# Weight pieces of 1024 columns in buffers of half the size, for a hybrid attention and convolution layer

## The chip, the core and the metric

The kernel runs on one core of one Trainium2 chip. The metric is device time in microseconds (us) of one execution; less is better. The core has a matrix engine (PE, whose weight loads are listed apart as PEld), a vector engine (DVE), a scalar engine (ACT), a general engine (POOL) and a queue that issues transfers (SP). Each takes its own instructions strictly in order, and semaphores tie them together. Transfers from all queues run on the same 16 DMA engines.

## The reference

One layer on 256 tokens of width 2048, all in float32, with batch 1 and depth 1:

```python
parts = split(x @ w_in)                        # q, k, v of 3 dilated groups, GLA's q, k, v, r, low, two gates
for g, dil in enumerate((1, 4, 16)):           # 8 heads of 128, span 128, T5 bias
    outs[g], lses[g] = dilated_group(q, k, v, bias, dil)
ya = (softmax(lses) * outs).sum() @ w_proj_a
log_a = log_sigmoid(g_low @ gla_gate_w + gla_gate_b) / 16
o = gla(gq, gk, gv, log_a)                     # 4 heads, chunks of 64
yb = (rms_norm(o) * gla_norm_g * silu(gr)) @ w_proj_b
x1 = layernorm(alpha * x + (sigmoid(m_a) * ya + sigmoid(m_b) * yb) @ w_out)
g = causal_conv3(x1 @ ffn_w_gate) + conv_b     # width 5632
out = layernorm(alpha * x1 + (silu(g) * (x1 @ ffn_w_up)) @ ffn_w_down)
```

Almost all of the work is x @ W with weights that are read once.

## The kernel before

**Pieces.** The host lays the weights out as a stream `wp` of pieces of 128 partitions x 2048 columns of float32 (1 MB each), in the order of `_stream`. `load` (L145 to L148) issues the transfer of one piece on SP, at L147. The PE multiplies float32 in a rounded form, so `split` (L135 to L137) makes two parts of each piece: ACT writes `hi`, a rounded copy (L136), and DVE writes `lo = raw - hi` (L137). A product of x and W is then three products, x_hi W_hi, x_lo W_hi and x_hi W_lo, summed in PSUM. `two_parts` and `piece` (L150 to L173) take the buffers.

**Buffers.** All are slots of 2048 columns: 2 of tag `raw` and 6 of tag `quarter` for loaded pieces, 3 of `whi` and 2 of `wlo` for the parts. A load can be issued when the piece that held its slot was read for the last time; for `raw` that is DVE's `lo`.

**Three ways to use a piece.**
- A *tile* (`b16`, L235): one piece holds 16 blocks of 128 columns as stationary operands. 16 matmuls of 512 columns use `hi` (L228), then 16 of 256 columns use `lo` (L230). The `gqk`, `qk`, `fg` and `fu` tiles are of this kind.
- A *chunk* (`chunk_step`, L264; `a_part`, L251): one piece holds four row blocks of 512 output columns, as moving operand, with 24 matmuls (L260, L261, L262). The `m`, `pb`, `yp`, `wo` and `wd` products are of this kind, with one piece for each step.
- A *unit* (`seven`, L312): a product of 256 rows in 2x2 blocks, with seven block products in place of eight. Each of the block products `p1` to `p7` uses two pieces and 24 matmuls (L329). Before `p5` and `p6` DVE adds pieces to pieces in place (`add`, L342); for `p7` and `p2` POOL issues adding transfers between buffers (`add_by_dma`, L345). There are 10 units in the mixer (`v`, `gv`, `gr`, `m`) and five in the feed-forward part (`fgu`).

**What sets the order.** The Python code names work in the order of use. In the mixer, steps of units are taken in turn with the tiles that make q and k; attention and GLA stages are put between them by `pump`. In the feed-forward part the blocks of 8, 8, 8, 8, 8, 4 row blocks (`FSPLIT`) run one after the other, and the `wd` steps of one block are put between the steps of the next one's unit. A scheduling layer then places the instructions of each engine, with its own estimate of when each can start, and adds the semaphores. So the order on ACT and DVE is close to that of the code, but not the same.

**Places that the prediction speaks of.** `vD`: in a unit, `p7` makes `u = s + E` (L378) and `c = D - u` (L379) on DVE, and `p3` then adds another product into the bank `D`, so PE waits for L379. `wd` after a unit: ACT copies the last bank of the unit (`c`, L398) and then splits the next `wd` piece. `fguA`: the second product into bank A, whose pieces ACT splits behind two transfers of `x1f` (L114) that ACT issues itself. `pa` (L982): the sum of a tile's two halves, which frees the tile's bank.

Of the kernel before, what the change touches and what calls it, by code (L numbers as in the profile page):

```python
# [11 lines left out]
F32 = mybir.dt.float32  # L12
# [22 lines left out]
NEG = -1e30  # L35
FSPLIT = (8, 8, 8, 8, 8, 4)


# [19 lines left out]
def hybrid_layer(ctx: ExitStack, tc: tile.TileContext, wp, xt, wgl, gw, par, relb, onehot, rows, xk, out):  # L58
# [91 lines left out]
    def two_parts(raw, spare=False):  # L150

        n_blk[0] += 1
        hi = wpool.tile([P, 2048], F32R, tag="quarter" if spare else "whi", name=f"whi_{n_blk[0]}", bufs=6 if spare else 3)
        lo = wpool.tile([P, 2048], F32R, tag="quarter" if spare else "wlo", name=f"wlo_{n_blk[0]}", bufs=6 if spare else 2)
        split(hi, lo, raw)
        return hi, lo

    def piece(i, before=(None,)):

        if len(before) == 1:  # L160
            return two_parts(load(i))
        raw = raw_tile(i)
        n_blk[0] += 1
        hi = wpool.tile([P, 2048], F32R, tag="whi", name=f"whi_{n_blk[0]}")
        lo = wpool.tile([P, 2048], F32R, tag="wlo", name=f"wlo_{n_blk[0]}", bufs=2)
        n = 2048 // len(before)
        for k, f in enumerate(before):
            if f is not None:
                f()
# [62 lines left out]

    by_cols = lambda ws: lambda kc: [a[:, kc * P : (kc + 1) * P] for a in ws]

    def b16(name, opnd, i, before=(None,)):  # L235
        return b_tile(name, by_cols(piece(i, before)), opnd, 16)

    def b16_three(names, opnd, idx):

        ws = [by_cols(two_parts(load(i), spare=(i == idx[-1]))) for i in idx]  # L240
        pss = [cbank(n) for n in names]
        for kc in range(16):
            for w, ps in zip(ws, pss):
                nc.tensor.matmul(ps, w(kc)[0], opnd(kc), start=(kc == 0), stop=False)
        for w, ps in zip(ws, pss):
            for kc in range(16):
                nc.tensor.matmul(ps[:, S:], w(kc)[1], opnd(kc)[:, :S], start=False, stop=(kc == 15))
        return pss
# [31 lines left out]
    def a_pair_by_half(name, opnd, idx):  # L280

        pcs = [piece(i) for i in idx]
        pss = [[cbank(f"{name}_t{t}") for t in range(2)] for _ in pcs]
        for t in range(2):
            for (hi, lo), ps in zip(pcs, pss):
                for k in range(4):
                    w = slice(k * 512, (k + 1) * 512)
                    a_part(ps[t], opnd(k), hi[:, w], lo[:, w], t, k == 0, k == 3)
        return pss
# [25 lines left out]
    def seven(name, xs, comb, i, store, by_dma=True):  # L315
# [7 lines left out]
        def part(ps, a, raw, p, first):  # L323

            hi, lo = two_parts(raw)
            for w, which in ((hi, 0), (hi, 1), (lo, 0)):
                for k in range(4):
                    kc = 4 * p + k
                    nc.tensor.matmul(  # L329
                        ps, a(kc)[which], w[:, k * 512 : (k + 1) * 512],  # L330
                        start=(first and w is hi and which == 0 and kc == 0),
                        stop=(w is lo and kc == 7), skip_group_check=not first,
                    )
# [13 lines left out]
        def get(k):  # L347
            return load(i + k, "quarter", 6)

        def p1():  # L350
            st["T"] = [get(0), get(1)]
            st["A"] = cbank(name + "A")
            product(st["A"], a11, st["T"])
            st["s"] = blk("s")
            nc.scalar.activation(st["s"], st["A"], AF.Copy)

        def p5():
            st["B12"] = [get(2), get(3)]
            for a, b in zip(st["T"], st["B12"]):
                add(a, b)  # L360
            st["D"] = cbank(name + "D")
            product(st["D"], z, st["T"])

        def p6():
            st["B22"] = [get(4), get(5)]
# [26 lines left out]
        def p2():  # L392
            st["B21"] = [get(6), get(7)]
# [4 lines left out]
            nc.scalar.activation(c, st["A"], AF.Copy)  # L398
            store(0, 0, c)
# [120 lines left out]
    def gkq(which, h):  # L520
        st = {}

        def f(j, before=(None,)):
            def g():
                ps = b16("gqk", xop, AT["gkq", which] + 2 * h + j, before)
                if not j:
                    st["b"] = blk("gqk")
                b_sum(ps, st["b"][:, j * S : (j + 1) * S])
                if j:
                    GKQ[which][h] = spill("gkqs", st["b"])  # L530
            return g
        return f

    def head(h):
# [3 lines left out]
        def f(g, which):  # L538
            def t():
                ps = b16("qk", xop, AT["qk", h] + 2 * g + which)  # L540
                if not which:
# [186 lines left out]
    def gkq_tiles():  # L728
        for which in range(2):
            for h in range(GH):  # L730
                f = gkq(which, h)
                yield f(0, [pair_of_x(j) for j in range(4)] if not which and not h else (None,))
                yield f(1)
# [102 lines left out]
    for n in range(2):  # L836
        pss = a_chunk("m", xop, 16, AT["mb"] + 4 * n, 2)
        for t in range(2):
# [3 lines left out]
    drain()  # L842
    home[:] = "quarter", 6
    early.close()
# [28 lines left out]
    for n in range(4):  # L873
        g = [gate(1, n, t) for t in range(2)]
        pss = a_chunk("pb", by_pairs(OB), 16, AT["pb"] + 4 * n)
        for t in range(2):
# [4 lines left out]
    for n in range(4):  # L881
        g = [gate(0, n, t) for t in range(2)]
        pss = a_chunk("yp", yop, 8, AT["pa"] + 2 * n)
        for t in range(2):
# [59 lines left out]
    for n in range(4):  # L944
# [3 lines left out]
        if n < 3:  # L948
            pss = a_chunk("wo", yt, 16, AT["wo"] + 4 * n)
            for t in range(2):  # L950
                residual(n, t, pss[t])
    pcs = [two_parts(load(AT["wo"] + 12 + k), spare=(k > 1)) for k in range(4)]
    for t in range(2):
        ps = cbank(f"wo_t{t}")
        for k0 in range(4):
            hi, lo = pcs[k0]
            for k in range(4):
                w = slice(k * 512, (k + 1) * 512)
                kc = 4 * k0 + k
                a_part(ps, yt(kc), hi[:, w], lo[:, w], t, kc == 0, kc == 15)  # L960
# [38 lines left out]
    def tile_group(f0, h):  # L999
# [3 lines left out]
        def gate_tile(f):  # L1003
            def g():
                if f == 0:
                    first = AT["fgu", 0]
                    st["three"] = dict(zip("gun", b16_three(("fg", "fu", "fg"), x1op, (first, first + 1, first + 2))))
                three = st.get("three", {})
# [4 lines left out]
        def up_tile(f):  # L1013
            def g():
                if f == 0:
                    ps = st["three"]["u"]
                elif f == 1:
                    with tc.issue_after(held.ins):
                        ps = b16("fu", x1op, AT["fgu", f] + 1)
                else:  # L1020
                    ps = b16("fu", x1op, AT["fgu", f] + 1)
                gated(h()[:, f % 4], st["c"], b_own(ps))
# [26 lines left out]
    def down_group(part, nf, hs):  # L1049
# [25 lines left out]
        def step(n, k0):  # L1075
            def g():
                at = AT["wd", part] + n * nf // 4
                if not k0:
# [17 lines left out]
        for n in range(0, 4, 2):  # L1096
            at = [AT["wd", part] + n + i for i in range(2)]
            if n == 2:
# [27 lines left out]

    home[:] = "raw", 2
    f0, older = 0, []
# [58 lines left out]
def _stream():  # L1187
# [129 lines left out]
```

## Time and profile before

| | |
|---|---|
| time, median of 3 runs | 1923.15 us (1919.91 to 1925.47) |
| the profiled execution, its own time | 1920.82 us |
| its span, first to last instruction | 1919.1 us |
| DVE, ACT, POOL busy | 1413.8, 1022.8, 179.6 us |
| mean granted PE clock | 0.985 |
| HBM read, written | 383.46 MB, 33.72 MB |
| transfers of pieces from HBM | 163 into `raw`, 160 into `quarter`, 1 MB each |

The profile lists busy time by engine, groups of instructions by line with their mean duration, waits (who waited for whom), a timeline, the time of DMA transfers, and the clock that the PE was granted, 1.00 being full speed. A busy PE is modelled: its matmuls overlap, so the pitch between them (0.227 us for 512 columns) is less than the 0.39 us that one is listed with. A wait is listed at the first instruction that could not start, with the instruction that released it.

### The profile page before, as it was taken

The numbers are of one execution on the slowest core, as the hardware profiler recorded it, in microseconds if no ns is written. First come the engines' busy times: TensorE is split into PE (matmuls) and PEld (weight loads), VectorE is DVE, ScalarE is ACT, GpSimd is POOL, SyncE is SP. The second block draws the span as 40 slices with busy tenths as digits, with TensorE's granted clock in tenths as the row PEclk, the third lists the DMA queues.
The fourth block names the chain that finished last, engine by engine and source line by source line (L and its number), as shares of the span: only waits on it lengthen the run. The fifth ranks groups of instructions, "written<-read, shape, count | busy, mean of one in ns | idle before, by whom it ended". The sixth has DMA issues, their size and how long they took to land.

```text
span 1919.1 us, 22883 instructions
## 1 busy us (share of the span) xinstructions
PE 1834.4 (96%) x8974; PEld 1530.1 (80%) x8974; DVE 1413.8 (74%) x1258; ACT 1022.8 (53%) x987; POOL 179.6 (9%) x289
## 2 busy tenths in 40 slices
PE   8998999999999999997999999899999999999996
PEld 6876888888888788885788868787887887887875
DVE  6867898887788786954656566685686885876977
ACT  5644675566565656544633445554554654554552
POOL 0001000101010101102200000000010010010111
PEclk9999999999999999999999999999999999999998
DMA  8887987978979788787656436569579587686783
GB/s 302 261 276 229 306 270 249 335 222 275 310 238 327 225 276 301 232 315 252 258 198 224 165 133 253 200 206 314 196 215 341 176 257 307 200 286 259 221 261 143
DMA packets 93319, 480.44 MB, mean 250 GB/s; under 512 B 11777, under 2 KB 24092, under 8 KB 44188
## 3 DMA queue, kind: packets, MB, share of 16 engines
q1 hardware_dynamic: 50252, 345.06, 47.7%
q0 software_dynamic: 24816, 115.47, 23.7%
q10 hardware_dynamic: 18144, 18.46, 3.1%
q8 instruction: 70, 1.15, 0.2%
q14 instruction: 37, 0.30, 0.0%
HBM read 383.46 MB, written 33.72 MB: 217 GB/s over the span
## 4 chain that ended last, share of the span: by engine, by line
PE 64%; issue 11%; DMA 11%; DVE 9%; ACT 3%; POOL 1%; ACTq 0%; SPq 0%; POOLq 0%; DVEq 0%
PE qk L228 7%; DVE wlo L137 5%; PE qk L230 4%; DMA raw<-in_wp 3%; PE wd_t L261 3%; PE wd_t L262 3%; PE wd_t L260 3%; PE fu L228 3%; PE fg L228 3%; PE fguA L329 2%; ACT whi L136 2%; DMA quarter<-in_wp 2%; PE fguD L329 2%; PE fguE L329 2%; PE fu L230 1%
## 5 line engine op out<-in xcount | busy, mean ns | idle before, releaser
L137 DVE TENSOR_TENSOR wlo<-quarter,whi 128x2048 fp32r<-128x2048 f32 x250 | 571.1, 2289 | 198.9 <-ACT whi L136 98.8
L136 ACT ACTIVATE whi<-quarter 128x2048 fp32r<-128x2048 f32 x250 | 477.6, 1916 | 353.8 <-DVE quarter L342 84.8
L136 ACT ACTIVATE whi<-raw 128x2048 fp32r<-128x2048 f32 (+1 forms) x167 | 314.2, 1884 | 285.7 <-DMA raw<-in_wp 130.9
L137 DVE TENSOR_TENSOR wlo<-raw,whi 128x2048 fp32r<-128x2048 f32 (+1 forms) x167 | 375.8, 2250 | 110.9 <-ACT whi L136 70.9
L228 PE MATMUL qk<-x,whi 128*128 128x512 f32 x768 | 191.8, 398 | 0.0
L228 PEld LDWEIGHTS qk<-x,whi 128*128 128x128 f32 x768 | 142.1, 188 | 29.7 <-issue 1.4
L261 PE MATMUL wd_t<-wlo,h 128*128 128x512 f32 x352 | 139.7, 397 | 5.5 <-DVE wlo L137 5.5
L260 PE MATMUL wd_t<-whi,h 128*128 128x512 f32 x352 | 138.0, 396 | 5.2 <-ACT whi L136 3.4
L342 DVE TENSOR_TENSOR quarter<-quarter,quarter 128x2048 f32<-128x2048 f32 x60 | 137.0, 2285 | 2.6 <-DMA quarter<-in_wp 2.1
L262 PE MATMUL wd_t<-whi,h 128*128 128x512 f32 x352 | 138.9, 395 | 0.0
L345 POOL DMA_DIRECT2D quarter<-quarter x60 | 52.7, 884 | 684.5 <-DMA quarter<-in_wp 150.6
L230 PEld LDWEIGHTS qk<-x,wlo 128*128 128x128 f32 x768 | 98.6, 191 | 4.3 <-DVE wlo L137 0.5
L230 PE MATMUL qk<-x,wlo 128*128 128x256 f32 x768 | 100.3, 283 | 0.1
L228 PE MATMUL fg<-x,whi 128*128 128x512 f32 x352 | 87.7, 403 | 6.9 <-DVE pa L982 6.9
L228 PE MATMUL fu<-x,whi 128*128 128x512 f32 x368 | 88.7, 393 | 1.2 <-DVE pa L982 1.2
L261 PEld LDWEIGHTS wd_t<-wlo,h 128*128 128x128 f32 x352 | 67.2, 191 | 21.8 <-DVE wlo L137 7.7
L260 PEld LDWEIGHTS wd_t<-whi,h 128*128 128x128 f32 x352 | 67.2, 191 | 20.9 <-ACT whi L136 4.7
L228 PEld LDWEIGHTS fg<-x,whi 128*128 128x128 f32 x352 | 66.6, 194 | 20.8 <-DVE pa L982 7.3
L228 PEld LDWEIGHTS fu<-x,whi 128*128 128x128 f32 x368 | 67.5, 188 | 14.6 <-ACT whi L136 1.4
L262 PEld LDWEIGHTS wd_t<-whi,h 128*128 128x128 f32 x352 | 67.2, 191 | 14.0 <-DVE h L137 0.2
L228 PE MATMUL gqk<-x,whi 128*128 128x512 f32 x256 | 64.2, 402 | 6.3 <-ACT whi L136 6.3
L228 PEld LDWEIGHTS gqk<-x,whi 128*128 128x128 f32 x256 | 48.6, 194 | 19.5 <-ACT whi L136 9.6
(361 smaller groups left out, 3127.0 us busy)
## 6 DMA issues: line engine op xcount, KB each, us to landing
raw<-in_wp SPq DMA_DIRECT2D x163, 1024.0 KB, 6.3
quarter<-in_wp SPq DMA_DIRECT2D x160, 1024.0 KB, 9.2
quarter<-quarter POOLq DMA_DIRECT2D x60, 1024.0 KB, 11.4
af<-acc POOLq DMA_DIRECT2D x32, 256.0 KB, 8.4
acc<-af POOLq DMA_DIRECT2D x32, 256.0 KB, 5.4
sp<-c POOLq DMA_DIRECT2D x14, 256.0 KB, 11.3
bias<-bvd ACTq DMA_DIRECT2D x32, 96.0 KB, 6.7
v<-vs ACTq DMA_DIRECT2D x24, 128.0 KB, 5.5
```

Source lines behind the costliest of these rows:

```text
L136: nc.scalar.activation(hi, src, AF.Copy)
L137: nc.vector.tensor_tensor(lo, src, hi.bitcast(F32), op=ALU.subtract)
L228: nc.tensor.matmul(ps, parts(kc)[0], opnd(kc), start=(kc == 0), stop=False)
L230: nc.tensor.matmul(ps[:, S:], parts(kc)[1], opnd(kc)[:, :S], start=False, stop=(kc == nk - 1))
L260: nc.tensor.matmul(ps, xh, hi, start=first, stop=False)
L261: nc.tensor.matmul(ps, xh, lo, start=False, stop=False)
L262: nc.tensor.matmul(ps, xl, hi, start=False, stop=last)
L329: nc.tensor.matmul(ps, a(kc)[which], w[:, k * 512 : (k + 1) * 512], start=(first and w is hi and which == 0 and kc == 0), stop=(w is lo an ...
L342: tt(a, a, b, op=ALU.add)
L345: nc.gpsimd.dma_start(a, b, accum_op=ALU.add)
```

## The change

Every piece is cut in two. A piece is now 128 x 1024 (`PC`), 512 KB, and each tag has twice the slots: 4 `raw`, 12 `quarter`, 6 `whi`, 4 `wlo`. The memory is the same. The weights, the matmuls (number, shape and operands) and the sums in PSUM are the same; a tile now takes its 16 blocks from two pieces, a chunk step asks for a new piece after two of its four blocks, and a block product of a unit runs over four pieces. Inside a piece of a unit the three passes (x_hi W_hi, x_lo W_hi, x_hi W_lo) are now of 2 matmuls each where they were of 4. The first tile, whose piece was loaded and split in four slices of 512 columns between loads of x, still is.

```diff
+PC = 1024
-    home = ["raw", 2]
+    home = ["raw", 4]
-        return wpool.tile([P, 2048], F32, tag=tag, name=f"{tag}_{i}", bufs=bufs)
+        return wpool.tile([P, PC], F32, tag=tag, name=f"{tag}_{i}", bufs=bufs)
...
-        hi = wpool.tile([P, 2048], F32R, tag="quarter" if spare else "whi", name=f"whi_{n_blk[0]}", bufs=6 if spare else 3)
-        lo = wpool.tile([P, 2048], F32R, tag="quarter" if spare else "wlo", name=f"wlo_{n_blk[0]}", bufs=6 if spare else 2)
+        hi = wpool.tile([P, PC], F32R, tag="quarter" if spare else "whi", name=f"whi_{n_blk[0]}", bufs=12 if spare else 6)
+        lo = wpool.tile([P, PC], F32R, tag="quarter" if spare else "wlo", name=f"wlo_{n_blk[0]}", bufs=12 if spare else 4)
...
-    by_cols = lambda ws: lambda kc: [a[:, kc * P : (kc + 1) * P] for a in ws]
+    def by_cols(pcs):
+        return lambda kc: [a[:, (kc % 8) * P : (kc % 8 + 1) * P] for a in pcs[kc // 8]]
-    def b16(name, opnd, i, before=(None,)):
-        return b_tile(name, by_cols(piece(i, before)), opnd, 16)
+    def b16(name, opnd, i, before=(None, None)):
+        n = len(before) // 2
+        pcs = [piece(i + k, before[k * n : (k + 1) * n]) for k in range(2)]
+        return b_tile(name, by_cols(pcs), opnd, 16)
...
     def chunk_step(pss, opnd, nk, i, k0):
-        hi, lo = piece(i + k0 // 4)
         for k in range(4):
             kc = k0 + k
-            w = slice(k * 512, (k + 1) * 512)
+            if not k % 2:
+                hi, lo = piece(i + kc // 2)
+            w = slice((k % 2) * 512, (k % 2 + 1) * 512)
...
             for w, which in ((hi, 0), (hi, 1), (lo, 0)):
-                for k in range(4):
-                    kc = 4 * p + k
+                for k in range(2):
+                    kc = 2 * p + k
...
         def get(k):
-            return load(i + k, "quarter", 6)
+            return [load(i + 4 * k + p, "quarter", 12) for p in range(4)]
         def p1():
-            st["T"] = [get(0), get(1)]
+            st["T"] = get(0)
...
     def b(w, c, rows=2048):
-        out.append((w, 0, rows, c, P))
+        for k in range(0, rows, 1024):
+            out.append((w, k, 1024, c, P))
     def a(w, c, first, rows):
-        for k in range(first, first + rows, 512):
-            out.append((w, k, 512, c, 512))
+        for k in range(first, first + rows, 256):
+            out.append((w, k, 256, c, 512))
```

The rest of the diff is the same for `a_pair_by_half`, the last `wo` chunk and the indices into the stream.

How this moves work on the engines is shown at three places. The lines after the change are numbered higher by 1 to 6 (L137 becomes L138, L379 becomes L385).

On DVE, at the first `vD` of the mixer, before the change; `wlo` are the low parts, `u`, `c` and `s` the block sums of the unit:

```order
L137 TENSOR_TENSOR wlo_874<-quarter_750,whi_873 128x2048
L378 TENSOR_TENSOR u_868<-s_611,vE_835 128x512
L137 TENSOR_TENSOR wlo_890<-quarter_752,whi_889 128x2048
L379 TENSOR_TENSOR c_104_869<-vD_672,u_868 128x512
L384 TENSOR_TENSOR s_611<-vD_672,s_611 128x512
```

And the same place after it:

```order
L138 TENSOR_TENSOR wlo_1007<-quarter_837,whi_1006 128x1024
L384 TENSOR_TENSOR u_981<-s_668,vE_940 128x512
L138 TENSOR_TENSOR wlo_1017<-quarter_839,whi_1016 128x1024
L385 TENSOR_TENSOR c_123_982<-vD_741,u_981 128x512
L138 TENSOR_TENSOR wlo_1031<-raw_1028,whi_1030 128x1024
```

Between `u` and `c` stands one low part, now of half the width.

On ACT, at the end of the second feed-forward unit, before the change; `c` is the copy of bank A, and the `whi<-raw` behind it are the high parts of `wd` pieces:

```order
L136 ACTIVATE whi_10907<-quarter_10447 128x2048
L398 ACTIVATE c_1258_10853<-fguA_10449 128x512
L136 ACTIVATE whi_10928<-raw_10926 128x2048
L136 ACTIVATE whi_10958<-raw_10956 128x2048
L136 ACTIVATE whi_11008<-raw_11006 128x2048
```

After it:

```order
L137 ACTIVATE whi_12770<-quarter_12192 128x1024
L404 ACTIVATE c_1573_12696<-fguA_12194 128x512
L137 ACTIVATE whi_12785<-raw_12783 128x1024
L137 ACTIVATE whi_12803<-raw_12801 128x1024
L137 ACTIVATE whi_12821<-raw_12819 128x1024
L137 ACTIVATE whi_12839<-raw_12837 128x1024
```

The copy `c` still stands ahead of all of them, and the first high part behind it is half as wide.

On ACT, ahead of the second product into bank A (`fguA`) of the first feed-forward unit, before the change; the two `whi<-quarter` are that product's high parts, `x1f` are transfers that ACT issues:

```order
L114 DMA x1f_9788<-x1s_8469 128x512
L136 ACTIVATE whi_9794<-raw_9792 128x2048
L114 DMA x1f_9790<-x1s_8592 128x512
L136 ACTIVATE whi_9836<-quarter_9830 128x2048
L136 ACTIVATE whi_9852<-quarter_9832 128x2048
```

After it:

```order
L115 DMA x1f_11435<-x1s_9938 128x512
L137 ACTIVATE whi_11459<-raw_11457 128x1024
L137 ACTIVATE whi_11495<-quarter_11483 128x1024
L115 DMA x1f_11437<-x1s_10061 128x512
L137 ACTIVATE whi_11505<-quarter_11485 128x1024
L137 ACTIVATE whi_11515<-quarter_11487 128x1024
L137 ACTIVATE whi_11525<-quarter_11489 128x1024
```

The first quarter of the product's high parts now stands ahead of the second transfer.

More of the change, by code (lines that the diff above doesn't have):

```diff
@@ L163, in piece @@
         n_blk[0] += 1
-        hi = wpool.tile([P, 2048], F32R, tag="whi", name=f"whi_{n_blk[0]}")
-        lo = wpool.tile([P, 2048], F32R, tag="wlo", name=f"wlo_{n_blk[0]}", bufs=2)
-        n = 2048 // len(before)
+        hi = wpool.tile([P, PC], F32R, tag="whi", name=f"whi_{n_blk[0]}", bufs=6)
+        lo = wpool.tile([P, PC], F32R, tag="wlo", name=f"wlo_{n_blk[0]}", bufs=4)
+        n = PC // len(before)
         for k, f in enumerate(before):
-            if f is not None:
-                f()
+            f()
             c = slice(k * n, (k + 1) * n)
@@ L521, in gkq, with f @@
         st = {}
-        def f(j, before=(None,)):
+        def f(j, before=(None, None)):
             def g():
-                ps = b16("gqk", xop, AT["gkq", which] + 2 * h + j, before)
+                ps = b16("gqk", xop, AT["gkq", which] + 2 * (2 * h + j), before)
                 if not j:
@@ L731, in gkq_tiles @@
                 f = gkq(which, h)
-                yield f(0, [pair_of_x(j) for j in range(4)] if not which and not h else (None,))
+                yield f(0, [pair_of_x(j) for j in range(4)] if not which and not h else (None, None))
                 yield f(1)
@@ L842, in hybrid_layer @@
     drain()
-    home[:] = "quarter", 6
+    home[:] = "quarter", 12
     early.close()
@@ L1006, in g @@
                     first = AT["fgu", 0]
[L1007 removed]
+                    st["three"] = dict(zip("gun", b16_three(("fg", "fu", "fg"), x1op, (first, first + 2, first + 4))))
                 three = st.get("three", {})
@@ L1096, in down_group @@
         for n in range(0, 4, 2):
-            at = [AT["wd", part] + n + i for i in range(2)]
+            at = [AT["wd", part] + 2 * (n + i) for i in range(2)]
             if n == 2:
@@ L1125, in sums @@
         return [get, lambda: part1(j)]
-    home[:] = "raw", 2
+    home[:] = "raw", 4
     f0, older = 0, []
```

39 lines of the change are left out of this document (20 added, 19 removed).

## Prediction

> **What bounds the kernel now.** I read the engines' totals first.
>
> ```profile
> PE 1834.4 (96%) x8974; PEld 1530.1 (80%) x8974; DVE 1413.8 (74%) x1258; ACT 1022.8 (53%) x987; POOL 179.6 (9%) x289
> ```
>
> PE is the bound: no more than its idle time and its slow time can be won, unless its work changes, and it doesn't. What there is to win stands in two views: who PE waited for, and where its clock was halved. The view of PE's waits (us in total, times, longest):
>
> ```profile
> PE pt L787 <- DVE sg L820: 9.8, 1, 9.8
> PE fg L228 <- DVE pa L982: 6.9, 2, 4.6
> PE gqk L228 <- ACT whi L136: 6.3, 3, 4.4
> PE wd_t L261 <- DVE wlo L137: 5.5, 3, 1.8
> ...
> PE vD L329 <- DVE c L379: 3.7, 1, 3.7
> PE gqk L230 <- DVE wlo L137: 3.6, 2, 3.3
> PE wd_t L260 <- ACT whi L136: 3.4, 3, 2.0
> ...
> PE fguA L329 <- ACT whi L136: 2.6, 1, 2.6
> PE vB L329 <- DVE wlo L137: 2.4, 2, 1.4
> PE pb_t L261 <- DVE wlo L137: 2.0, 2, 1.7
> ...
> PE mB L329 <- DVE wlo L137: 1.4, 2, 1.2
> ...
> PE gvB L329 <- DVE wlo L137: 1.2, 1, 1.2
> ...
> PE vA L329 <- DVE wlo L137: 1.0, 1, 1.0
> ```
>
> Waits for `whi` and `wlo` are waits for a piece that is being split: the change can shorten these. `pt` waits for data of GLA at a stage's end: that isn't touched. Next, stretches at half clock (length; PE, PEld, DVE, ACT, POOL busy; clock, DMA share, GB/s). These are four of the nine, and the sum of the nine:
>
> ```profile
> 1315.62:1319.03 3.41, 3.18 (x8) 2.51 (x9) 3.20 (x2) 3.41 (x3) 0.00 (x0) 0.50 0.67 276
> 1469.22:1472.63 3.41, 3.41 (x10) 2.63 (x9) 1.81 (x1) 0.00 (x0) 0.00 (x0) 0.50 1.02 418
> 1602.34:1605.75 3.41, 3.41 (x10) 2.64 (x9) 1.94 (x1) 0.00 (x0) 0.03 (x1) 0.50 1.00 396
> 1735.46:1738.87 3.41, 2.96 (x7) 2.41 (x8) 3.19 (x3) 0.00 (x0) 0.00 (x0) 0.50 1.00 351
> sum 44.37, PE 36.96 PEld 29.30 DVE 30.31 ACT 18.76 POOL 6.93; mean PE 4.11 PEld 3.26 DVE 3.37 ACT 2.08 POOL 0.77
> ```
>
> Each of these four follows one of the waits above, of `fguA` or of `wd`, and a stretch of 3.41 us at half clock costs 1.7 us on top of the wait.
>
> **What a half piece costs.** The groups by shape (busy, mean ns | idle before), then two DVE splits back to back in the timeline (start, length):
>
> ```profile
> L137 DVE TENSOR_TENSOR wlo<-quarter,whi 128x2048 fp32r<-128x2048 f32 x250 | 571.1, 2289 | 198.9 <-ACT whi L136 98.8 <-issue 27.5 <-PE wo_t L261 15.6
> L137 DVE TENSOR_TENSOR wlo<-raw,whi 128x2048 fp32r<-128x2048 f32 x163 | 373.0, 2289 | 110.0 <-ACT whi L136 70.1 <-PE fg L247 9.0 <-PE m_t L261 5.2
> L136 ACT ACTIVATE whi<-raw 128x2048 fp32r<-128x2048 f32 x163 | 311.7, 1914 | 284.7 <-DMA raw<-in_wp 130.0 <-PE wd_t L262 44.1 <-PE qk L228 34.9
> L342 DVE TENSOR_TENSOR quarter<-quarter,quarter 128x2048 f32<-128x2048 f32 x60 | 137.0, 2285 | 2.6 <-DMA quarter<-in_wp 2.1
> L137 DVE TENSOR_TENSOR wlo<-raw,whi 128x512 fp32r<-128x512 f32 x4 | 2.8, 691 | 0.9 <-ACT whi L136 0.9
> L136 ACT ACTIVATE whi<-raw 128x512 fp32r<-128x512 f32 x4 | 2.5, 630 | 1.0 <-DMA raw<-in_wp 0.9
> ```
>
> ```profile
> 317.15 4.49 DVE L137 TENSOR_TENSOR wlo<-quarter,whi 128x2048 fp32r<-128x2048 f32 x2
> ```
>
> DVE: 691 ns for 512 columns and 2289 for 2048 give 1.040 ns a column, so 1224 ns for 1024. ACT: 630 and 1914 give 1058 ns. So the first half of a low part is ready 1.06 us sooner and that of a high part 0.86 us sooner. A second start adds 159 ns on DVE and 202 on ACT by duration. Back to back it may be less: two DVE splits take 4.49 us, a pitch of 2.20, which leaves 0.07 us beyond the columns. DVE has 250 + 163 + 60 = 473 such instructions: +33 us by pitch to +75 us by duration. ACT's 413: +83 us. Beside 1413.8 and 1022.8 us in a span of 1919.1 this makes 78% and 58%, and it lies under PE's work wherever an engine is ahead of PE. Without that cover it is the slow rival below.
>
> SP issues 323 more loads, at 0.33 us each, 106 us; POOL issues 60 more adding transfers, between nothing and another 53 us in all:
>
> ```profile
> L147 SPq DMA_DIRECT2D raw<-in_wp x163: 327/328/493, 10.9 to 1883.2; - x163
> L345 POOL DMA_DIRECT2D quarter<-quarter x60 | 52.7, 884 | 684.5 <-DMA quarter<-in_wp 150.6
> ```
>
> SP does nothing else for most of the span, and POOL is 9% busy and sat 684.5 us idle ahead of these, so I cost both at nothing on the path. Without that cover, a transfer queued behind them on POOL (spills and fetches of 256 KB) starts up to 1.8 us later.
>
> **Waits that shrink.**
>
> ```profile
> 1463.50 0.60 ACT L398 ACTIVATE c<-fguA 128x512 f32<-128x512 f32 x1 [7.66 <-DMA acc<-af]
> 1464.00 1.91 ACT L136 ACTIVATE whi<-raw 128x2048 fp32r<-128x2048 f32 x1
> 1465.94 2.29 DVE L137 TENSOR_TENSOR wlo<-raw,whi 128x2048 fp32r<-128x2048 f32 x1 [2.86 <-ACT whi L136]
> ...
> 1465.96 0.51 PE L260 MATMUL wd_t<-whi,h 128*128 128x512 f32 x1 [0.29 <-ACT whi L136]
> ...
> 1468.28 0.50 PE L261 MATMUL wd_t<-wlo,h 128*128 128x512 f32 x1 [1.82 <-DVE wlo L137]
> ```
>
> This is the `wd` place. ACT is held at `c` by a transfer that frees its buffer; then the split of the next piece runs bare, hi and lo one after the other. With halves, hi comes 0.86 and lo another 1.06 us sooner. A half holds 12 of the 24 matmuls, 2.7 us of PE (half of the product shown next), and the second half's parts follow at 1.06 and 1.22 us, so nothing is late behind it. What remains is `c`'s own wait.
>
> - `wd` L261, 3 times: 3 x 1.06 = 3.2. L260, 3 times (2.0, the 0.3 shown, so 1.1): 0.3 + 0.86 + 0.86 = 2.0.
> - `fguA` 2.6: the first quarter of its high parts now stands ahead of the transfer it was held by; the second doesn't. A quarter is 6 matmuls, 1.4 us, so about 0.4 remains: 2.2.
> - `gqk` L230 3.3 and 0.3: 1.06 + 0.3 = 1.3. `pb` 1.7 and 0.3: 1.3. `vA` 1.0: 1.0. `gqk` L228: 5.6 of its 6.3 is the first tile, which stays in slices of 512; the rest, 0.7, goes.
>
> Together 11.7. On DVE's queue: at `vD` a half low part stands ahead of `c` now, 1.06 sooner. At the two `pa` waits a low part stood ahead of the sum too, and in the new order a half one does: 2.1. Together 3.2. With these, the `wd` waits fall to 0.8 to 1.9 us and `fguA` to 0.4; `pb`'s 1.7 was followed by no slow stretch, so I let the four slow stretches go: 4 x 1.7 = 6.8.
>
> The Trainium skill, "TensorE: Matmul & The Clock Gate", section "What's actually happening", says that the clock halves after at least one idle window of about 3.4 us; by that alone the `wd` waits, all shorter, would not have cost a stretch and the 5.1 us of the three would not be in the sum. The three rows at 0.50 say otherwise here.
>
> **Where nothing is won.** `vB`, `mB` and `gvB` (5.0 us, 5 times) come in products ahead of which DVE adds two pieces and then splits two.
>
> ```profile
> 192.77 5.47 PE vD L329 x24
> ```
>
> That is 4 x 2.29 = 9.2 us of DVE for a product of 5.47 us. In halves it is 8 x 1.22 = 9.8 us: the start comes sooner, the end 0.3 (by pitch) to 0.6 us later. The bounds are all 5.0 us gone, and 30 such products (60 adds by twos) each 0.64 later, +19. I take 5 x 0.45 = +2.3, since only the five that wait now are without cover.
>
> **Sum.** -11.7 - 3.2 - 6.8 + 2.3 = -19.4 against the profiled execution's 1920.8 (its span of 1919.1 and 1.7 around it): 1901.4. The median of the runs is 2.3 above that execution, so the forecast is **1904 us**, 1.0% faster. A measurement of this kernel tells 0.3%, about 6 us, from no change.
>
> **Rivals.**
> - *More is won.* Twice the slots of half the size let DVE and ACT run half a piece further ahead, and every wait for a piece outside the first tile goes (23.8 us of the rows above), with those of `vD` and `pa` (10.6) and six slow stretches (10.2). Together 44.6: 1879. Against it: `c` and `pa` are held by other things too.
> - *No change.* The three slow stretches after `wd` show a DMA share of 1.00 to 1.02: the transfers are at their limit there. If a sooner first half only meets a later second half, or the schedule's new order brings new waits, the 15 us of shorter waits come back and the clock stretches stay: 1918 to 1928, say 1922.
> - *Slower, by DVE.*
>
> ```profile
> 48.00:96.00 48.00, 48.00 (x254) 40.89 (x253) 43.14 (x39) 29.09 (x27) 3.42 (x5) 1.00 0.82 261
> 240.00:288.00 48.00, 46.56 (x233) 38.66 (x233) 44.70 (x43) 34.34 (x33) 4.54 (x7) 1.00 0.83 271
> ...
> 768.00:816.00 48.00, 48.00 (x245) 40.72 (x244) 44.00 (x36) 26.79 (x23) 5.13 (x7) 1.00 0.79 231
> ```
>
>   DVE is busy 44.7 of 48 us in the second of these stretches. Some 15 wide instructions gain 0.07 to 0.16 us each, 1 to 2.4 us, so it comes to 47 and stays just below PE. It decides from 48 on: then each of the 30 products with adds ends 0.64 later, 19.2, with three new slow stretches, 5.1, and half of the 14.9 us of shorter waits kept: +17, 1940. Against it: in the two others DVE is busy 43 and 44 us, and PE is busy for all 48.
> - *Slower, by the loads.*
>
> ```profile
> raw<-in_wp SPq DMA_DIRECT2D x163, 1024.0 KB, 6.3
> ...
> out<-acc SPq DMA_DIRECT2D x7, 256.0 KB, 2.5
> ```
>
>   A `raw` slot now turns in 6.3 + 1.9 + 2.3 = 10.5 us, two slots give a piece every 5.25 us, and PE takes one in 5.47. With four slots and a half load of L us it is (L + 2.28) / 2; L lies between 2.5 (256 KB) and 6.3 (1 MB), so 2.4 to 4.3 us. Feed gets worse only from L = 8.2. If a half load took 9.2, pieces would come every 5.74 us, and 0.27 on 163 pieces is 44; with a third of them bare, +15: 1938.
>
>   The Trainium skill, "DMA: Bandwidth & Descriptors", section "Rules for kernel authors", speaks against the change: at least 1 MiB a transfer for the most bandwidth. Its fit of 2.0 us + bytes / 436 GB/s (section "Anatomy of one DMA") gives an estimate of 3.2 us for 512 KB where 1 MB takes 4.4; by it the sum would stay as it is.
>
> **How the numbers follow.** Forecast 0.54, more won 0.10, no change 0.17, slower by DVE 0.13, by the loads 0.06. So faster by over 0.3% 0.64, within 0.3% 0.17, slower 0.19. The range of 1882 to 1938 leaves out the far ends of the first rival and of the two slow ones. The forecast's own range is 1888 to 1916.
>
> **What would show it.** Right: 128x1024 splits of about 1.22 and 1.06 us; `wd` waits under 1 us at L261 and no 0.50 stretch behind them; `fguA` under 1; DVE 1450 to 1490 us busy. Wrong: PE waits for `wlo` in the B and D products of units in sum over 10 us (DVE), or ACT's waits for `raw` loads above the present 130 us (loads); and with neither, the half clock still behind the `wd` steps.

## The result, and the profile after

| | before | after |
|---|---|---|
| time, median | 1921.63 us (1919.91 to 1925.47, 4 runs) | 1904.51 us (1900.0 to 1908.64, 4 runs) |
| ratio, 95% interval | | 0.9908, 0.9879 to 0.9936 |
| the profiled execution, its span | 1920.82, 1919.1 us | 1908.64, 1906.9 us |
| the same comparison again, with more runs | 1919.33 us (11 runs) | 1906.19 us (6 runs), ratio 0.9934, 0.992 to 0.9949 |

The two ratios give 17.7 and 12.7 us. The kernel is faster, by 0.7 to 0.9%.

The totals after (busy, share of the span, instructions), then the groups by shape (busy, mean ns of one | idle before):

```profile
PE 1834.6 (96%) x8974; PEld 1533.4 (80%) x8974; DVE 1455.2 (76%) x1731; ACT 1092.1 (57%) x1400; POOL 236.4 (12%) x349
...
L138 DVE TENSOR_TENSOR wlo<-quarter,whi 128x1024 fp32r<-128x1024 f32 x500 | 598.2, 1220 | 191.4 <-PE qk L230 39.3 <-issue 38.4 <-ACT whi L137 32.3
L137 ACT ACTIVATE whi<-raw 128x1024 fp32r<-128x1024 f32 x326 | 342.2, 1057 | 271.6 <-DMA raw<-in_wp 109.8 <-PE wd_t L266 56.4 <-PE qk L228 27.3
L351 POOL DMA_DIRECT2D quarter<-quarter x120 | 105.0, 894 | 685.0 <-ACT whi L137 242.8 <-DMA quarter<-in_wp 137.4 <-DVE quarter L348 136.0
```

A split of 1024 columns takes 1220 ns on DVE and 1057 on ACT, where 1224 and 1058 had been worked out. DVE is busy 41 us longer in all, inside the 33 to 75 forecast. An adding transfer of half the size costs POOL as much to issue as a whole one (894 against 884 ns), so the upper bound of 53 us came true. PE's work is the same to 0.2 us. What changed is whom it waited for (us in total, times, longest):

```profile
PE pt L793 <- DVE sg L826: 9.3, 1, 9.3
PE fg L228 <- DVE af L1073: 9.2, 3, 3.6
PE fg L228 <- DVE pa L988: 6.2, 3, 3.9
...
PE gqk L228 <- ACT whi L137: 3.6, 2, 2.9
PE ps L468 <- DVE s L470: 3.4, 2, 2.2
...
PE wd_t L264 <- DVE af L1073: 2.8, 1, 2.8
PE vD L335 <- DVE wlo L138: 2.6, 2, 2.1
PE vB L335 <- DVE wlo L138: 2.0, 1, 2.0
PE mB L335 <- DVE wlo L138: 1.7, 2, 1.2
PE gvB L335 <- DVE wlo L138: 1.5, 1, 1.5
...
PE vD L335 <- DVE c L385: 0.7, 1, 0.7
```

All waits of `wd_t` for `whi` and `wlo` are gone (8.9 us before), and with them those of `fguA`, `pb_t`, `vA` and the low parts of `gqk`; `vD` for `c` went from 3.7 to 0.7. The second row is new, with the same count, three, as the `wd` places. The rows of the whole view sum to 57.7 us, against 67.5 before. Here is the first of the three new places, on ACT, DVE and PE (start, length; idle before in brackets):

```profile
1455.04 1.06 ACT L137 ACTIVATE whi<-raw 128x1024 fp32r<-128x1024 f32 x1 [0.82 <-DMA raw<-in_wp]
1463.37 1.06 ACT L137 ACTIVATE whi<-raw 128x1024 fp32r<-128x1024 f32 x1 [7.28 <-DMA raw<-in_wp]
```

```profile
1464.47 3.74 DVE L138 TENSOR_TENSOR wlo<-raw,whi 128x1024 fp32r<-128x1024 f32 x3 [7.11 <-ACT whi L137]
1468.12 0.68 DVE L1073 TENSOR_TENSOR af<-af,wd_t 128x512 f32<-128x512 f32 x1
```

```profile
1468.95 0.76 PE L228 MATMUL fg<-x,whi 128*128 128x512 f32 x1 [3.44 <-DVE af L1073]
```

The `wd` steps have run through, but the `fg` tile behind them takes one of the two banks that the `wd` tiles use, and `af` on DVE frees it. `af` stands behind three splits of pieces that land 7 us late. The DMA engines were busy nearly all of the time then, with a share of 1.03 from 1440 to 1455 us and this in the ten after it:

```profile
1455.00:1465.00 10.00, 10.00 (x46) 8.23 (x45) 2.83 (x4) 2.47 (x3) 1.08 (x2) 1.00 0.97 386
```

So the wait stands one tile later than the `wd` waits did before. The half clock is found there too: these are the two stretches behind the new waits, and the sum of all eleven (length; PE, PEld, DVE, ACT, POOL busy; clock, DMA share, GB/s), against nine stretches and 44.37 us before.

```profile
1467.81:1474.64 6.83, 5.69 (x14) 4.46 (x15) 3.69 (x6) 3.17 (x5) 1.09 (x2) 0.50 0.91 314
1604.35:1607.76 3.41, 3.41 (x10) 2.64 (x9) 0.85 (x2) 1.75 (x3) 0.55 (x1) 0.50 0.80 284
...
sum 54.60, PE 45.24 PEld 35.04 DVE 38.97 ACT 29.57 POOL 11.97; mean PE 4.11 PEld 3.19 DVE 3.54 ACT 2.69 POOL 1.09
```

The loads changed as well. The queue of SP: its waits for earlier loads to land before it could issue, before and after, and the issues after (count, KB, median us to landing).

```profile
SPq L147 <- DMA raw<-in_wp: 64.2, 27, 7.5
...
SPq L147 <- DMA quarter<-in_wp: 7.0, 2, 4.5
```

```profile
SPq L148 <- DMA quarter<-in_wp: 98.0, 58, 6.1
SPq L148 <- DMA raw<-in_wp: 48.6, 26, 5.6
...
raw<-in_wp SPq DMA_DIRECT2D x326, 512.0 KB, 4.9
quarter<-in_wp SPq DMA_DIRECT2D x320, 512.0 KB, 7.1
```

Half a `raw` piece lands in 4.9 us where a whole one took 6.3. But SP now waits 98 us for `quarter` loads to land, in 58 places, where it waited 7 us in two. For `raw` loads it waits less, 49 us against 64; together these waits went from 71 to 147 us. The program's own list of SP's transfers shows what it waits for, here some rows of the changed kernel:

```
315 L148 DMA raw_7730<-in_wp 128x1024 [waits DMAHW4_49,DVE_49]
316 L148 DMA raw_7748<-in_wp 128x1024 [waits DMAHW5_49,DVE_49]
317 L148 DMA quarter_8433<-in_wp 128x1024 [waits DMAHW6_49,DVE_49]
318 L148 DMA quarter_8451<-in_wp 128x1024 [waits DMAHW7_49,DVE_49]
319 L148 DMA quarter_8473<-in_wp 128x1024 [waits DMAHW0_49,DVE_49]
```

The scheduling layer marks the landing of SP's and ACT's transfers with eight semaphores in turn, DMAHW0 to DMAHW7, and a transfer can be issued only when the last one with its semaphore has landed. So no more than eight are under way. In the trace, of the transfers issued from 1425.40 us on, the ninth was issued at 1442.22, when the first had landed at 1442.15; the tenth at 1443.49, the second having landed at 1443.42. Eight whole pieces were all the slots of before (2 `raw`, 6 `quarter`). Eight halves are half of that, whatever number of slots there is. Neither this limit nor its price was in the prediction.

### The profile page after: what moved, and what is told of

Same layout as the page of the kernel before. It is cut to its first block, busy times and chain, and to the rows that moved or that the text cites. A ratio compares the mean times of both kernels' runs of the same rounds, so it can differ in the third digit from the quotient of the medians.

```text
span 1906.9 us, 25497 instructions
## 1 busy us (share of the span) xinstructions
PE 1834.6 (96%) x8974; PEld 1533.4 (80%) x8974; DVE 1455.2 (76%) x1731; ACT 1092.1 (57%) x1400; POOL 236.4 (12%) x349
## 3 DMA queue, kind: packets, MB, share of 16 engines
q1 hardware_dynamic: 96764, 345.09, 50.5%
## 4 chain that ended last, share of the span: by engine, by line
PE 70%; DMA 10%; DVE 7%; issue 5%; ACT 2%; POOL 1%; ACTq 0%; DVEq 0%; POOLq 0%; SPq 0%
PE qk L228 7%; DMA raw<-in_wp 4%; PE qk L230 4%; DVE wlo L138 3%; PE fg L228 3%; PE fu L228 3%; PE wd_t L264 3%; PE wd_t L266 3%; PE wd_t L265 3%; PE fguA L335 3%; PE fguD L335 3%; PE fguE L335 2%; DMA quarter<-in_wp 2%; PE mE L335 2%; PE pb_t L264 2%
## 5 line engine op out<-in xcount | busy, mean ns | idle before, releaser
L138 DVE TENSOR_TENSOR wlo<-quarter,whi 128x1024 fp32r<-128x1024 f32 x500 | 598.2, 1220 | 191.4 <-PE qk L230 39.3
L137 ACT ACTIVATE whi<-quarter 128x1024 fp32r<-128x1024 f32 x500 | 522.9, 1057 | 299.0 <-DVE quarter L348 49.9
L137 ACT ACTIVATE whi<-raw 128x1024 fp32r<-128x1024 f32 (+1 forms) x330 | 344.7, 1052 | 271.9 <-DMA raw<-in_wp 110.0
L138 DVE TENSOR_TENSOR wlo<-raw,whi 128x1024 fp32r<-128x1024 f32 (+1 forms) x330 | 394.4, 1213 | 97.0 <-ACT whi L137 40.8
L228 PE MATMUL qk<-x,whi 128*128 128x512 f32 x768 | 192.3, 399 | 0.0
L351 POOL DMA_DIRECT2D quarter<-quarter x120 | 105.0, 894 | 685.0 <-ACT whi L137 242.8
L228 PEld LDWEIGHTS qk<-x,whi 128*128 128x128 f32 x768 | 141.8, 188 | 29.4 <-issue 1.4
L348 DVE TENSOR_TENSOR quarter<-quarter,quarter 128x1024 f32<-128x1024 f32 x120 | 142.5, 1215 | 0.3
L228 PE MATMUL fg<-x,whi 128*128 128x512 f32 x352 | 92.6, 419 | 15.4 <-DVE af L1073 9.2
L228 PEld LDWEIGHTS fg<-x,whi 128*128 128x128 f32 x352 | 69.9, 203 | 31.5 <-ACT whi L137 9.8
L228 PE MATMUL fu<-x,whi 128*128 128x512 f32 x368 | 88.7, 393 | 0.6 <-DVE pa L988 0.6
L228 PEld LDWEIGHTS fu<-x,whi 128*128 128x128 f32 x368 | 67.5, 188 | 14.0 <-issue 0.7
L228 PE MATMUL gqk<-x,whi 128*128 128x512 f32 x256 | 68.0, 419 | 3.6 <-ACT whi L137 3.6
L228 PEld LDWEIGHTS gqk<-x,whi 128*128 128x128 f32 x256 | 51.4, 205 | 17.7 <-ACT whi L137 7.1
```

The lines of the kernel that those rows point to most:

```text
L137: nc.scalar.activation(hi, src, AF.Copy)
L138: nc.vector.tensor_tensor(lo, src, hi.bitcast(F32), op=ALU.subtract)
L228: nc.tensor.matmul(ps, parts(kc)[0], opnd(kc), start=(kc == 0), stop=False)
L348: tt(a, a, b, op=ALU.add)
L351: nc.gpsimd.dma_start(a, b, accum_op=ALU.add)
```

## Experiments

Theories: **S**, the gain is in the splits; **L**, it is in the loads; **B**, what `wd` won came back at the bank of `fg`; **N**, the number of transfers under way costs. Other letters are explained in the text that stands ahead of each result.

### The changed kernel again

> The changed kernel as it is, once more with more rounds, for a tighter interval and a second profile. The forecast's terms as they came out give about 0.991 of the time before (17 us of 1921.6 in the first comparison). Two things are asked of the profile. Theory T (the gain at the wd places is handed to the fg tile behind them, which needs a PSUM bank that af on VectorE frees): the waits of fg for af stay, 8 to 10 us over 3 places, and 0.50 stretches stand right behind them. Rival (one execution's chance): they are elsewhere, or fewer than 4 us in sum.

1906.19 us, ratio 0.9934 (0.992 to 0.9949). The wait for the bank is there, just under the 8 to 10 us expected, and SP's waits are too (100.3 us for `quarter` loads, 54.1 for `raw`):

```profile
PE fg L228 <- DVE af L1073: 7.8, 3, 3.5
```

The half clock sums to 44.36 us in nine stretches here, the same as before the change. Only one of them (at 1599.6 us) stands behind a wait of `fg` for `af`, so that part of theory T failed. The waits recur from one execution to the next; which of them costs a stretch doesn't.

### Half splits, whole loads

From the kernel before: transfers of 1 MB into slots of 2048 columns, split by halves into half-size parts.

```diff
+        his, los = [], []
+        for k in range(2):
+            his.append(wpool.tile([P, 1024], F32R, tag="whi", name=f"whi_{n_blk[0]}_{k}", bufs=6))
+            los.append(wpool.tile([P, 1024], F32R, tag="wlo", name=f"wlo_{n_blk[0]}_{k}", bufs=4))
+            split(his[k], los[k], raw[:, k * 1024 : (k + 1) * 1024])
```

> Half of the change alone: 1 MB loads and 2048-column raw slots as before, but both splits are made on 1024-column halves into twice as many whi and wlo buffers of half the size. Theory S (the gain is in the splits: 1.2 us in place of 2.4 us until the first half can be used, and half-size buffers that come free earlier): most of the gain is here, 8 to 14 us below the kernel before, 0.993 to 0.996, and PE's waits for whi and wlo at the wd tiles fall from 8.9 us to under 4. Theory L (the gain is in the loads: a half piece lands 1.4 us sooner, 4.9 against 6.3 us): within 4 us of the kernel before, and the wd waits stay over 6 us.

1899.48 us, ratio 0.9899 (0.988 to 0.9918): 19.4 us, more than the whole change and more than the 8 to 14 that S expected. PE's waits:

```profile
PE fg L244 <- DVE af L1083: 11.7, 3, 4.1
...
PE wd_t L277 <- DVE wlo L146: 1.8, 2, 1.4
```

S holds by the time, with loads as they were. The waits at `wd` for parts fell from 8.9 to 1.8 us, but this proves little: they fall without half splits too (see the smaller packets below). The wait at the bank of `fg` came here as well.

### Half loads, whole splits

```diff
-        nc.sync.dma_start(raw, wp[i])
+        for k in range(2):
+            c = slice(k * 1024, (k + 1) * 1024)
+            nc.sync.dma_start(raw[:, c], wp[i, :, c])
```

> The other half alone: each 1 MB piece is loaded by two 512 KB transfers into its 2048-column slot, and the splits are whole as before. The split needs both transfers, so nothing can start sooner; SyncE issues 413 more transfers. Theory S: no change, within 4 us of the kernel before. Theory L: part of the gain, if it comes from smaller transfers sharing the DMA engines better: 5 us or more below. Rival (smaller transfers cost the DMA engines more): 5 us or more above.

1946.14 us, ratio 1.0153 (1.0128 to 1.0179): the rival, by 29 us. SP issues 323 more transfers here, not 413. SP's waits and ACT's (ACT waited 130.9 us for `raw` loads before):

```profile
SPq L149 <- DMA raw<-in_wp: 105.1, 55, 5.8
SPq L149 <- DMA quarter<-in_wp: 97.0, 56, 6.8
```

```profile
L136 ACT ACTIVATE whi<-raw 128x2048 fp32r<-128x2048 f32 (+1 forms) x167 | 314.7, 1884 | 325.4 <-DMA raw<-in_wp 178.8
```

### Smaller packets, one transfer per piece

Half loads differ from whole ones in two things: packets of 4096 B for 8192, and twice the number of transfers. Here the weights lie as in the changed kernel, and one transfer brings both halves.

```diff
-        nc.sync.dma_start(raw, wp[i])
+        nc.sync.dma_start(raw.rearrange("p (t c) -> p t c", t=2), wp[i].rearrange("t p c -> p t c"))
```

> The kernel before, with its weights laid out in DRAM as the change lays them out: each 1 MB piece is still one transfer into one 2048-column slot, but out of two blocks of 512 KB, so in packets of 4096 B instead of 8192 B. It tells apart why two half transfers per piece cost 27 us. Theory N (the number: a transfer of SyncE cannot be issued before the eighth one ahead of it has landed, so half-size transfers halve the bytes under way): within 5 us of the kernel before, and SyncE's waits for quarter<-in_wp stay near the 7 us over 2 places of before (half loads: 97 us over 56). Theory K (the packets: the share of the hardware queue rises from 47.7 to about 50 per cent and everything lands later): 12 to 30 us slower than the kernel before.

1920.86 us, ratio 1.0022 (1.0003 to 1.004). SP's wait, and the queue (packets, MB, share):

```profile
SPq L147 <- DMA quarter<-in_wp: 7.7, 3, 4.6
```

```profile
q1 hardware_dynamic: 91596, 345.06, 49.1%
```

By the ratio the packets cost 4 us, 8 at most. So of the 29 us of half loads some 25 are not theirs. SP's waits stay near those of before (for `raw` loads 76.0 us against 64.2), where half loads had brought both rows to about 100. The number of transfers is what is left.

This run shows one thing more. Its splits are whole, and its order of instructions is the same on every engine as in the kernel before. Still PE waits elsewhere:

```profile
PE fg L228 <- ACT gc L989: 10.7, 3, 3.7
...
PE wd_t L261 <- DVE wlo L137: 1.6, 4, 0.8
```

The waits at `wd` for parts fell from 8.9 to 1.6 us and three waits of `fg` behind the `wd` steps came in, with no gain in time. At the first of them ACT's `gc` stands behind the split of a piece for which ACT had waited 7.0 us. So with whole splits, too, a late piece can show at `wd` or at `fg`, and the two profiles before and after don't by themselves show that the change moved the wait.

### Twice the transfers, nearly the same bytes

From the half splits with whole loads.

```diff
-        nc.sync.dma_start(raw, wp[i])
+        for c in (slice(0, 2040), slice(2040, 2048)):
+            nc.sync.dma_start(raw[:, c], wp[i, :, c])
```

> The half splits with 1 MB transfers, where each piece is loaded by two transfers instead of one, of 2040 and of 8 columns: nearly the same bytes in nearly the same packets, and twice the number of transfers. Theory N (a transfer waits for the landing of the eighth one ahead of it, so that twice the number halves the bytes under way): 7 to 27 us slower than the half splits alone, about 0.994 to 1.004 of the kernel before, and SyncE's waits for quarter<-in_wp rise from 7 us to over 50. Rival Z (it is the even halves that cost, since the second half lands late, or the packets): within 5 us of the half splits alone.

1910.59 us, ratio 0.9954 (0.994 to 0.9968), against 0.9899 for the half splits alone: 10.6 us slower.

```profile
SPq L157 <- DMA quarter<-in_wp: 104.0, 48, 7.1
SPq L157 <- DMA raw<-in_wp: 86.9, 44, 5.9
```

N holds: SP's waits for `quarter` loads rose from 7.1 us to 104.0 and those for `raw` from 62.6 to 86.9, with no load cut in half. The packets are not the same, though: the queue has 96764 against 50252, the added ones small, and its share rose from 48.0 to 49.4%, as much as with the smaller packets. By the 4 us that those cost (8 at most), an estimate is that some 6 of the 11 us are the number's, 3 at the least. On whole splits it was some 25; why less here wasn't tried. Nor was a kernel with more than eight transfers under way: that the number costs through this limit is read from SP's waits and not shown by a run of its own.

### Half splits, whole buffers

```diff
-        split(hi, lo, raw)
+        for c in (slice(0, 1024), slice(1024, 2048)):
+            split(hi[:, c], lo[:, c], raw[:, c])
```

> The kernel before with its splits done on two halves of 1024 columns, but the whi and wlo buffers whole (three and two of 2048 columns), so that a half can be used as soon as it is split and a buffer comes free only when both halves have been used. Theory U (the gain of the half splits is the earlier first use): as with the half-size buffers, 0.988 to 0.993 of the kernel before. Theory F (it is the half-size buffers that come free earlier): within 6 us of the kernel before, or slower by VectorE's 33 us of added busy time.

1916.86 us, ratio 1.0 (0.9985 to 1.0016): theory F. PE's waits:

```profile
PE fg L229 <- DVE af L1068: 10.7, 3, 4.1
...
PE wd_t L262 <- DVE wlo L137: 0.8, 1, 0.8
```

In the program of this run PE's first matmuls on a piece wait for the split of its first half alone (for `wlo_94` at DVE's count of 89, one before that of the second half). So that half is used sooner, and yet nothing is won in all (DVE is busy 24 us longer than before the change, which is part of this balance). The step from here to half-size `whi` and `wlo`, with the same splits at the same 1220 ns, is worth 0.0101 of the time, 19 us. So it is the buffers that carry the gain: a half-size one can be written again as soon as its half of the matmuls is done. In the program here the first half of a new `whi` waits for the last matmul on the whole piece that held the buffer. ACT's waits for the `wd` matmuls that free `whi`, with whole buffers and with half-size ones:

```profile
ACT whi L136 <- PE wd_t L263: 48.1, 12, 4.3
```

```profile
ACT whi L145 <- PE wd_t L278: 66.3, 42, 2.1
```

The waits are shorter, 2.1 us at the longest against 4.3, though there are more of them and not less in sum. The scheduling layer also orders the splits differently in the two kernels, so the buffers aren't told apart from the order that they allow. Which of the two tags matters more wasn't tried.

### Other banks for `fg`

From the changed kernel: `fg` and `fu` behind the units take their bank from the pool of four.

```diff
-        ps = mbank(name)
+        ps = (banks or mbank)(name)
...
+ ... b16("fg", x1op, AT["fgu", f], banks=cbank if f >= 8 else None)
```

> The changed kernel, with one thing moved: the fg and fu tiles behind the units (f of 8 and over) take their PSUM bank from the pool of four (psc) instead of the pool of two (psm) that the wd tiles use. Theory B (what the wd places won came back at fg, which waits for the bank that af frees on VectorE): the waits of fg for af, 8 to 9 us over 3 places, are gone and the half-clock stretches behind them with them; 7 to 13 us below the changed kernel, 0.987 to 0.990 of the kernel before. Rival R (fg's own weights are as late as its bank, because the loads are late): the same places wait for whi or wlo instead, and the time stays within 4 us of the changed kernel.

1901.4 us, ratio 0.992 (0.9897 to 0.9943). No wait of `fg` for `af` is left, only that for `pa`, and from 1243.7 to 1892.2 us the clock is full throughout:

```profile
PE fg L228 <- DVE pa L988: 6.5, 3, 3.8
```

```profile
1243.70:1892.22 648.52, 637.35 (x3121) 535.75 (x3119) 513.34 (x602) 367.09 (x461) 82.01 (x122) 1.00 0.78 249
```

From the first `fg` matmul to the last of `wd` it took 737.1 us, against 746.4 and 744.0 in the two profiles of the changed kernel: 7 to 9 us less. Of the whole time B asked 7 to 13 us and a ratio of 0.987 to 0.990, and that was missed. The medians are 5 us apart and the intervals overlap, so a gain of the whole time is only likely.

### A busier DVE

```diff
         nc.vector.tensor_tensor(lo, src, hi.bitcast(F32), op=ALU.subtract)
+        if lo.shape[-1] == PC:
+            c = slice(0, 64)
+            nc.vector.tensor_tensor(lo[:, c], src[:, c], hi[:, c].bitcast(F32), op=ALU.subtract)
```

> The changed kernel, with VectorE made busier and nothing else: behind each 1024-column low part VectorE computes the first 64 columns of it a second time, the same values, some 826 instructions more (at 0.07 to 0.2 us each about 60 to 165 us of busy time, by the 0.05 us and more that a start costs in the pairs of halves). Theory C (VectorE's added starts are covered, as the forecast held): within 8 us of the changed kernel. Rival D (VectorE's queue sets the end at many places): slower by a fifth or more of the added busy time, 15 us and over.

1931.18 us, ratio 1.0074 (1.0051 to 1.0097), 25 us slower than the changed kernel: rival D.

```profile
PE 1833.7 (95%) x8974; PEld 1528.8 (79%) x8974; DVE 1569.4 (82%) x2557; ACT 1090.5 (57%) x1400; POOL 232.3 (12%) x349
```

```profile
PE fg L231 <- DVE af L1076: 16.2, 3, 6.0
```

DVE is busy 114 us longer, and 22% of it reaches the end. It shows first where DVE's queue holds a bank: the waits of `fg` for `af` doubled. But the repeat writes `lo` itself, so each low part is also ready 0.22 us later; the run doesn't tell this from the busier queue, and the 22% holds for the two together.

### Pieces of 512 columns

Edit: `PC = 512`, and every count of buffers doubled again.

> The change carried one step further: pieces of 512 columns, 256 KB each, in four times as many buffers of a quarter of the size. By the start of a VectorE instruction as the halves showed it (2 x 1219 ns against 2 x 1.22 from one of 2.4 us, so about 0.05 us each) VectorE gains about 60 us of busy time, ScalarE (two of 1057 ns against one of 1.95 us, 0.16 us each) some 130 us, both hidden; SyncE issues 826 more transfers. Theory T (what is left is late raw loads and the bank of fg, not the grain of the pieces): within 4 us of the changed kernel, about 1901 to 1908, with the waits of fg for af still at 5 to 10 us. Rival G (the finer the better, as the step before): 5 to 10 us faster than the changed kernel. Rival D (more, smaller transfers and more instructions): slower by over 6 us, with ACT's waits for raw above 130 us.

1930.33 us, ratio 1.0061 (1.0046 to 1.0076), 24 us slower than the changed kernel. It is rival D's time, not its sign: ACT's waits for `raw` loads fell to 84.4 us. DVE is busy 71.6 us longer (1526.8), which at 22% is an estimated 16 us; eight transfers under way now hold 2 MB.

```profile
SPq L148 <- DMA quarter<-in_wp: 177.0, 272, 3.4
```

```profile
PE ps L469 <- DVE s L471: 13.1, 5, 6.5
PE vB L336 <- DVE wlo L138: 7.9, 2, 4.8
```

How the 24 us divide between the two stays open.

### Half splits, whole loads and other banks

The two edits that gained, on the kernel before.

> The two edits that gained, together, as a version that may beat both kernels: the kernel before with half splits into half-size buffers and 1 MB transfers, and the fg and fu tiles behind the units in the pool of four banks. With the half splits alone 0.9899 of the kernel before, with the banks alone 5 us off the changed kernel. Theory A (the two add, since the half splits alone still show 11.7 us of waits of fg for af over 3 places): 5 to 12 us below the half splits alone, 0.984 to 0.988 of the kernel before. Rival (what fg gains is waited for at its weights): 0.988 to 0.992.

1896.04 us, ratio 0.9884 (0.9869 to 0.9898): the fastest kernel of the study by median. Beside the half splits alone (0.9899, 0.988 to 0.9918) it isn't told apart; the ratio lies in the rival's range, its interval in both, so the expectation is left undecided. Part of what `fg` no longer waits for is waited for at `wd`:

```profile
PE wd_t L277 <- DVE wlo L146: 8.3, 5, 2.3
```

## Why the prediction came out, point by point

- **The time.** 1904.0 was forecast, 1904.5 and 1906.2 were measured. The gain was forecast at 19 us and is 13 to 18. Against its own profiled execution (1920.8) the sum said 1901.4, and the two profiles of the changed kernel took 1908.6 and 1904.2. PE's waits fell by 9.8 us in the first of these, where the terms for waits make 12.6. The step to the median, +2.3, wasn't borne out: the kernel before has a median of 1918.0 over 22 runs, below its profiled execution, not above.
- **Durations and hidden work.** 1224 and 1058 ns were right to 4 ns. DVE's added 41 us were costed at nothing, and this failed: at the 22% of the busier DVE, an estimate is 9 us. The cover was judged by stretches where PE is busy all the time. But DVE's queue also frees banks, and there what stands ahead of `af` or `s` can reach the end.
- **Waits that shrink, 11.7, and DVE's queue, 3.2.** At their places the rows came true: `wd` L260 and L261, `fguA`, `pb_t`, `vA`, the low parts of `gqk` and `c` at `vD`. The two `pa` waits, 2.1, didn't (6.9 to 6.2), and `gqk` L228 fell by 2.7 where 0.7 was counted. What the sum missed is what was late next behind `wd`: the bank of `fg`, 9.2 and 7.8 us, as much as the 8.9 that went. The smaller packets made the same trade with whole splits, so these rows are no measure of what the halves won there.
- **Half clock, 6.8.** This is the term that failed outright: 44.37 us at half clock before, 54.60 and 44.36 after. The stretches moved to other waits.
- **Products with adds, +2.3.** Their 5.0 us became 9.1 (five rows of `vD`, `vB`, `mB`, `gvB` and `gvD` for `wlo`), 4.1 more.
- **What filled the gap.** The reason given was that a half piece is ready sooner. Half splits in whole buffers have just that and gain nothing in all; with half-size buffers they gain 19 us. The prediction put this under "more is won", as a rival. The half loads take back 7 of the 19 (0.9899 to 0.9934). So the size came out because the unseen gain of the buffers and the unseen costs of the transfers and of DVE nearly cancelled. That is luck; the direction was reasoned, though by the lesser of the two ways in which halves can help. Another 2.7 us lie behind the last `wd` matmul, 16.8 us from the end before and 14.1 after, and weren't in the sum.
- **The signs.** The four for "right" came: 1220 and 1057 ns, no row of `wd` for `wlo`, none of `fguA`, and DVE 1455.2 us busy. Of those for "wrong", PE's waits for `wlo` in B and D products sum to 9.1 us, just under 10, and ACT's for `raw` loads fell to 110.0. So the signs passed while the half clock did not follow, and the sign for the loads would have missed their cost.
- **The rivals.** "Slower, by the loads" named the right part and the wrong mechanism: the half loads are worth 29 us by themselves, although a half lands no later than a whole one did (6.2 against 6.3 us), and what counts is the number of transfers; SP's waits put that down to the eight that may be under way. The estimate of 3.2 us for half a load and 4.4 for a whole one fell short: the `raw` loads took 4.9 and 6.3. "No change" had the busy DMA engines at the `wd` places right. The Trainium skill's rule of at least 1 MiB a transfer ("DMA: Bandwidth & Descriptors", "Rules for kernel authors") gives the right direction here; the packet size, the nearest to a bandwidth effect, is worth 4 us.

## What to carry to other kernels

Cut the buffer where it is freed, and keep the transfer whole: one 1 MB load split into half-size buffers was faster than half-size loads into them. Before more and smaller transfers are issued, count how many may be under way at once, and look at the issuing queue's own waits for earlier transfers. When a wait of PE is gone from a profile, look for it at the next place before calling it won: in one run here it moved with no change of order at all. Ask which bank or buffer the next tile needs, and what stands ahead of its release.

## What the runs showed of the hardware

- While PE had matmuls left, the clock fell to 0.50 in stretches of 3.41 us or multiples of it, and the length of PE's wait doesn't say when. In the first profile after, 1.91 us of waiting for `pa` were followed by a stretch (1208.40 to 1211.81); in the second, 2.59 us for `af` were not (ten microseconds at 1.00 around it):

```profile
1207.14 0.74 PE L228 MATMUL fg<-x,whi 128*128 128x512 f32 x2 [1.91 <-DVE pa L988]
```

```profile
1730.77 0.70 PE L228 MATMUL fg<-x,whi 128*128 128x512 f32 x2 [2.59 <-DVE af L1073]
...
1730.00:1740.00 10.00, 9.23 (x50) 8.09 (x51) 5.24 (x10) 5.68 (x9) 1.09 (x2) 1.00 0.62 208
```

- POOL was busy, on average, 0.88 us for each adding transfer of 1 MB (52.7 us for 60) and of 512 KB (105.0 for 120), and 0.89 for 256 KB (214.3 for 240): it doesn't fall with the size.
- Packets of 4096 B in place of 8192, for the same bytes, raised the share of the loading queue from 47.7 to 49.1%.
